# An encoder block on one core: other buffers for gates and w_out, another order for the last routed tile

## The chip, the core and the metric

The kernel runs on one core of one Trainium2 chip. The core has a matrix engine (TensorE, PE), VectorE (DVE), ScalarE (ACT), GpSimd (POOL) and SyncE (SP), which here issues most of the transfers; 16 DMA engines move data between the main memory and the on-chip memory. The metric is the time of one execution on the device in microseconds (us). Shown are the median of three runs of the kernel before and one profiled run.

## What is computed

One layer of an encoder block on 1024 rows of 1024 numbers: two attention branches, whose outputs are gated and merged, then a mixture of 32 experts.

```python
proj = rms_norm(x, norm_mix) @ w_in      # latents, q k v, two gates g_mla, g_diff
o_mla = mla_branch(...)
o_diff = diff_branch(...)                # needs exp(lq1 . lk1) - exp(lq2 . lk2)
merged = sigmoid(g_mla) * (o_mla @ w_mla_up) + sigmoid(g_diff) * (o_diff @ w_diff_up)
x = x + merged @ w_out
h2 = rms_norm(x, norm_ffn)
# router: best of 4 groups, then best 2 of the 8 experts in it, for each row
x = x + sum(combine[:, e] * ((silu(h2 @ w_gate[e]) * (h2 @ w_up[e])) @ w_down[e]) for e in range(32))
```

## The kernel before

Every product in full precision is made of three matmuls (`mm3`, L85 to L89) on operands split into a high part (ScalarE, L83) and a low remainder (VectorE, L84). A weight slab is 128 x 1024 numbers, 512 KB. Slabs are loaded by SP into raw buffers: five called `er`, which serve the whole kernel in turn, some called `ex` for expert weights (`N_MORE` of them), and pairs from a pool called `ring` whose tiles hold other things before.

The stages, with their place in the span:

- Projections, up to about 253 us. Then attention, up to 677 us. `gates()` computes the 32 blocks of gate columns as filler between the attention matmuls: each block is evicted by ScalarE into `sg` and stored to `g_d` by a DMA that ScalarE issues (L494 to L496). `sg` has one buffer. At the start of attention the products of lq and lk are formed from small tiles `lq` and `lj` (L607 to L615, loads on GpSimd); the first differential head has its values loaded from `dv_d` into er(3) and er(4) (L630, GpSimd).
- Merge, to about 770 us: 8 column blocks (L787 to L815). `uhi` and `ulo` are the split weights, `sgl` the gates loaded back from `g_d`. Four slabs of w_out are loaded and split within it (`slab`), the last four (k = 4 to 7, `woh` and `wol`) after it. The raw buffer of slab k is er(2 + k % 3) by `load_wo`, so k = 7 takes the buffer that k = 4 leaves.
- w_out, residual and router, to 895 us: eight tiles of 128 rows (L1024 to L1053) in an order written out by hand for TensorE, VectorE and ScalarE. A tile has two column halves of 24 matmuls (`out_mm`); between its own matmuls stand the transposes (`x2_turn`), router products (`logits`), counting (`count`, in `route`) and placing (`place`) of the tile before. For each tile SP stores the sum to `out` and the normed rows to `h2_d` (`h_d` in the trace). Expert slabs are loaded beside it, `load_pairs(2)` after every second tile.
- Experts, to the end. `slot_lists` writes the row numbers `ids` (VectorE, L1063). The first three gather buffers are cleared by ScalarE (L1084), since a gather leaves rows without a token as they are. Per expert: an indirect load of 112 rows of `h_d` (GpSimd, L1111, up to 12 ahead), eight transposes (`tokens`), 24 matmuls (`gate_up`), `hidden_t`, 12 matmuls (`down`), and an indirect store that adds 112 rows to `out` (L1163). Each add waits for the one before. `weights` splits six slabs per expert and then reloads the buffer it has read, or, for ring pairs, gives the pair to the gather or output buffers while more than `R_RAW` slabs are on their way (L1091 to L1107).

Within TensorE, VectorE and ScalarE's queues and within SP's and GpSimd's each instruction waits for those ahead of it.

Of the kernel before, what the change touches and what calls it, by code (L numbers as in the profile page):

```python
# [22 lines left out]
D = 1024  # L23
NT = 8
# [13 lines left out]
NYB = 3  # L38
N_MORE = 4
GB = 9  # L40
# [8 lines left out]
def kernel(ctx: ExitStack, tc: tile.TileContext, a, out):  # L49
# [45 lines left out]
    nlam = cst.tile([P, 1], F32, name="nlam")  # L95
    pos = cst.tile([P, NT, 2], F32, name="pos")
    eid = cst.tile([P, NT, 2], F32, name="eid")
    c4 = cst.tile([P, NT, 2, 4], F32R, name="c4")
    slots = cst.tile([P, P], F32, name="slots")
    nc.gpsimd.iota(slots, pattern=[[1, P]], base=0, channel_multiplier=0, allow_small_or_imprecise_dtypes=True)  # L100
    dump = cst.tile([P, 1], F32, name="dump")
    nc.gpsimd.iota(dump, pattern=[[0, 1]], base=S, channel_multiplier=1, allow_small_or_imprecise_dtypes=True)
    ndump = cst.tile([P, 1], F32, name="ndump")
    nc.vector.tensor_scalar(ndump, dump, -1.0, None, op0=ALU.mult)
    cnt = cst.tile([P, NE], F32, name="cnt")

# [367 lines left out]
    def gates():  # L474

        for b in range(2 * KD):
            raw = er(0)
            nc.sync.dma_start(raw, a["w_gate"][b].rearrange("p k n -> p (k n)"))
            w = []
            for j in range(2):  # L480
                w.append([pg.tile([P, 512], F32R, name=n_, bufs=3) for n_ in ("whi", "wlo")])
                split(*w[j], raw[:, j * 512:(j + 1) * 512])
            for half in range(2):
                ps = bank(gate_bank[0])
                if len(gate_bank) > 1:
                    gate_bank.append(gate_bank.pop(0))
                o = half * 512
                for k in range(KD):
                    wh, wl = w[k // 4]
                    c = slice(k % 4 * P, (k % 4 + 1) * P)  # L490
                    mm3(ps, wh[:, c], wl[:, c], hTh[k][:, o:o + 512], hTl[k][:, o:o + 512], k == 0, k == KD - 1)
                    if k < KD - 1:
                        yield
                sg = pg.tile([P, 512], F32, name="sg", bufs=1)  # L494
                nc.scalar.activation(sg, ps, AF.Copy)  # L495
                nc.scalar.dma_start(g_d[b, :, o:o + 512], sg)  # L496
                yield
# [109 lines left out]

    lq = p2.tile([P, 4, DHD], F32, name="lq")
    for i, n_ in enumerate(("lq1", "lk1", "lq2", "lk2")):
        nc.gpsimd.dma_start(lq[:, i, :], bcast(a[n_], DHD))  # L610
    lj = p2.tile([P, DHD], F32, name="lj")
    ls = p2.tile([P, 2], F32, name="ls")
# [166 lines left out]
    def load_wo(hi, lo):  # L779
        raw = er(2 + len(wo) % (N_RAW - 2))  # L780
        nc.sync.dma_start(raw, a["w_out"][:, len(wo), :])
# [38 lines left out]
    es_ps.close()  # L820
    es_r = ExitStack()
    psF = es_r.enter_context(tc.tile_pool(name="psF", bufs=4, space=PSUM))
    pwo = es_r.enter_context(tc.tile_pool(name="pwo", bufs=1, **left))
# [61 lines left out]
    def out_mm(t, c, k0, k1):  # L885
# [8 lines left out]
        for k in range(k0, k1):  # L894
            c_ = slice(k * P, (k + 1) * P)
            mm3(ps, mT[t // 2][0][:, t % 2, c_], mT[t // 2][1][:, t % 2, c_], wo[k][0][:, o], wo[k][1][:, o], k == 0, k == KD - 1)

    def weighted(t, c):

# [3 lines left out]
    def x2_half(t, c):  # L903
# [9 lines left out]
        weighted(t, 1)  # L913
        nc.sync.dma_start(out[t * P:(t + 1) * P, :], x2)
        r = rt("r2", [P, 1])
# [4 lines left out]
    def normed(t):  # L920

        h2 = PS2.pop(t)[2]
        nc.scalar.activation(h2, h2, AF.Copy, scale=R2[t])
        nc.sync.dma_start(h2_d[t * P:(t + 1) * P, :], h2)

# [95 lines left out]
    for i in range(N_MORE):  # L1021
        load([pex.tile([P, 1024], F32, name=f"ex{i}")])
    with tc.manual_schedule(engines={mybir.EngineType.PE, mybir.EngineType.DVE, mybir.EngineType.Activation}):
        for t in range(NT):  # L1024
            if 1 < t + 1 < NT:
                residual(t + 1)
            out_mm(t, 0, 0, 3)
            if t:
                x2_turn(t - 1, 0)
                x2_turn(t - 1, 1)  # L1030
                normed(t - 1)
            out_mm(t, 0, 3, KD)
            if t:
                logits(t - 1, 0, KD)
            x2_half(t, 0)
            out_mm(t, 1, 0, 6)
            if t:
# [5 lines left out]
            if t:  # L1043
                place(t - 1)
            x2_half(t, 1)
            if t % 2:
                load_pairs(2)
        logits(t, 0, 4)
        x2_turn(t, 1)
        logits(t, 4, KD)  # L1050
        normed(t)
        acted = route(t)
# [4 lines left out]
    def slot_lists(ps, n, nm):  # L1057


        idf = cst.tile([P, n], F32, name=f"idf{nm}")  # L1060
        nc.vector.tensor_scalar(idf, ps[:, 3 * n:4 * n], ndump, dump, op0=ALU.mult, op1=ALU.add)
        ids = cst.tile([P, n], I32, name=f"ids{nm}")
        LISTED.append(nc.vector.tensor_tensor(ids, ps[:, :n], idf, op=ALU.add))  # L1063
        w = cst.tile([P, n], F32, name=f"wsl{nm}")
        nc.vector.tensor_copy(w, ps[:, n:2 * n])
# [14 lines left out]
    pe = ctx.enter_context(tc.tile_pool(name="pe", bufs=1, **left))  # L1080
    gbuf = [pe.tile([P, D], F32, name=f"g{i}") for i in range(NGB)]
    with tc.issue_after(acted.ins):
        for g_ in gbuf:
            nc.scalar.activation(g_.rearrange("p (k n) -> p k n", n=P), slots[:, None, :].to_broadcast([P, KD, P]),  # L1084
                                 AF.Copy, scale=0.0)
    gused = {}
# [243 lines left out]
```

## Time and profile before

| | |
|---|---|
| median of 3 runs | 1274.68 us (1271.69 to 1276.09) |
| profiled run | 1274.59 us |
| its span, first to last instruction | 1272.4 us |
| mean granted TensorE clock | 0.966 |
| PE busy | 1158.7 us, 91% of the span |
| DVE busy | 946.0 us, 74% |
| ACT busy | 746.7 us, 59% |
| POOL busy | 172.8 us, 14% |
| moved by DMA | 228.62 MB, mean 180 GB/s |

Busy times are sums over the whole span; the stages have different limits. A granted clock of 1.00 is 2.4 GHz, 0.50 is 1.2 GHz. The duration of one matmul in the profile overlaps that of the next; the distance between two starts is the time that one costs. In brackets stand the idle time of the engine before the instruction and what ended it. A line marked SPq or ACTq is an instruction of that engine's queue that issues a transfer; its duration is that of the issue.

### The profile page before, as it was taken

To read this page: it belongs to the slowest core of one execution; us is meant where nothing else is said; L and a number is where in the kernel's file an instruction comes from. 1 tells how busy PE (TensorE), PEld (TensorE's weight loads), DVE (VectorE), ACT (ScalarE), POOL (GpSimd) and SP (SyncE) were. 2 spreads that over 40 slices of the span, in tenths; PEclk is the share of its full clock that TensorE was granted. 3 is DMA by queue.
4 is the path that set the end of the run, shared out by engine and by line. 5 is a ranking of instruction groups with operands and counts; after the bars stand their busy time and mean duration, and the time that the engine had idled before them with its cause. 6 is when DMAs were issued, how large, how long until landed. Compare 5 with 4: busy or idle time off the path is not lost.

```text
span 1272.4 us, 18235 instructions
## 1 busy us (share of the span) xinstructions
PE 1158.7 (91%) x6105; PEld 946.7 (74%) x6105; DVE 946.0 (74%) x2099; ACT 746.7 (59%) x1400; POOL 172.8 (14%) x147
## 2 busy tenths in 40 slices
PE   7889999989999998999999999999399998788993
PEld 6778888868888886778777877888277766566772
DVE  4776783458888788888865775565599988778992
ACT  5544562356667677776663443323488877667881
POOL 1000000010000001111100000000155233423112
PEclk9989999999999999999999998999599999899997
DMA  8753475383232233431125446544769999999983
GB/s 254 230 176 108 116 195 161 101 181 94 81 92 75 75 112 88 116 116 51 66 95 195 141 140 254 184 166 156 235 209 338 298 316 319 311 301 332 355 302 51
DMA packets 107615, 228.62 MB, mean 180 GB/s; under 512 B 13984, under 2 KB 47392, under 8 KB 107520
## 3 DMA queue, kind: packets, MB, share of 16 engines
q1 hardware_dynamic: 81664, 193.59, 46.0%
q0 software_dynamic: 21248, 25.46, 9.7%
q10 hardware_dynamic: 4608, 8.39, 1.8%
q8 instruction: 49, 0.80, 0.3%
q14 instruction: 46, 0.38, 0.1%
HBM read 187.53 MB, written 52.43 MB: 189 GB/s over the span
## 4 chain that ended last, share of the span: by engine, by line
PE 47%; DMA 27%; DVE 12%; ACT 6%; issue 5%; POOL 1%; SPq 1%; POOLq 0%; ACTq 0%; DVEq 0%
PE pG L87 5%; PE pG L88 5%; PE pG L89 5%; DMA ring<-in_w_exp 5%; DMA ex<-in_w_exp 4%; DMA er<-in_w_exp 4%; PE pB L530 3%; DMA out<-ring,ids 3%; DMA sgl<-g_d 2%; PE pF L87 2%; PE pF L88 2%; PE pF L89 2%; PE pO L89 2%; DVE nbd L518 2%; PE pO L87 2%
## 5 line engine op out<-in xcount | busy, mean ns | idle before, releaser
L521 ACT ACTIVATE pd<-pA,nbd 128x512 f32<-128x512 f32 (+7 forms) x128 | 94.5, 739 | 39.1 <-DVE nbd L518 36.2
L87 PE MATMUL pG<-ring,whi 128*128 128x512 f32 x240 | 98.9, 412 | 4.8 <-ACT sg L495 4.7
L518 DVE TENSOR_REDUCE nbd<-pA 128x1 f32<-128x128 f32 (+7 forms) x128 | 95.7, 749 | 2.5 <-PE pA L569 1.5
L89 PE MATMUL pG<-ring,wlo 128*128 128x512 f32 x240 | 96.0, 400 | 0.0
L88 PE MATMUL pG<-ring,whi 128*128 128x512 f32 x240 | 95.7, 399 | 0.0
L84 DVE TENSOR_TENSOR elo<-er,ehi 128x1024 fp32r<-128x1024 f32 x70 | 82.9, 1221 | 8.6 <-ACT ehi L83 8.5
L84 DVE TENSOR_TENSOR elo<-ring,ehi 128x1024 fp32r<-128x1024 f32 x66 | 78.2, 1221 | 5.8 <-ACT ehi L83 5.8
L83 ACT ACTIVATE ehi<-er 128x1024 fp32r<-128x1024 f32 x70 | 72.4, 1057 | 16.5 <-DMA er<-in_w_exp 8.9
L83 ACT ACTIVATE ehi<-ring 128x1024 fp32r<-128x1024 f32 x66 | 69.0, 1059 | 17.1 <-PE pO L89 5.2
L84 DVE TENSOR_TENSOR elo<-ex,ehi 128x1024 fp32r<-128x1024 f32 x56 | 66.8, 1222 | 12.6 <-ACT ehi L83 12.4
L83 ACT ACTIVATE ehi<-ex 128x1024 fp32r<-128x1024 f32 x56 | 58.3, 1058 | 21.2 <-DMA ex<-in_w_exp 9.6
L87 PE MATMUL pG<-ehi,xh 128*112 128x512 f32 x128 | 53.2, 416 | 19.1 <-ACT xh L83 19.1
L530 PE MATMUL pB<-ident,pd 128*128 128x128 f32 x432 | 66.0, 277 | 1.9 <-DVE pd L573 0.9
L530 PEld LDWEIGHTS pB<-ident,pd 128*128 128x128 f32 x432 | 48.8, 141 | 12.5 <-PE pO L597 2.5
L89 PE MATMUL pB<-ehi,ehl 128*112 128x512 f32 x128 | 54.1, 423 | 3.4 <-DVE ehl L84 3.3
L87 PEld LDWEIGHTS pG<-ring,whi 128*128 128x128 f32 x240 | 45.6, 190 | 15.0 <-ACT sg L495 8.8
L87 PE MATMUL pB<-ehi,ehh 128*112 128x512 f32 x128 | 53.7, 420 | 0.7 <-DVE ring L1162 0.7
L1163 POOL DMA_INDIRECT out<-ring,ids x20 | 34.1, 1706 | 138.8 <-ACT esg L1134 45.0
L89 PEld LDWEIGHTS pG<-ring,wlo 128*128 128x128 f32 x240 | 45.8, 191 | 9.2 <-DVE wlo L84 0.2
L88 PE MATMUL pB<-elo,ehh 128*112 128x512 f32 x128 | 52.5, 410 | 0.0
L89 PE MATMUL pG<-ehi,xl 128*112 128x512 f32 x128 | 52.2, 408 | 0.0
L87 PE MATMUL pO<-ehi,xh 128*112 128x512 f32 x128 | 51.6, 403 | 0.6 <-ACT ehi L83 0.6
(395 smaller groups left out, 3574.9 us busy)
## 6 DMA issues: line engine op xcount, KB each, us to landing
er<-in_w_exp SPq DMA_DIRECT2D x70, 512.0 KB
ring<-in_w_exp SPq DMA_DIRECT2D x66, 512.0 KB
ex<-in_w_exp SPq DMA_DIRECT2D x56, 512.0 KB
er<-in_w_gate SPq DMA_DIRECT2D x16, 512.0 KB
g_d<-sg ACTq DMA_DIRECT2D x32, 256.0 KB
sgl<-g_d SPq DMA_DIRECT2D x32, 256.0 KB
er<-in_w_dqkv SPq DMA_DIRECT2D x8, 512.0 KB
xT<-in_xT SPq DMA_DIRECT2D x16, 256.0 KB
```

Of the source, the lines that this page charges most:

```text
L83: nc.scalar.activation(hi, src, AF.Copy)
L84: return (eng or nc.vector).tensor_tensor(lo, src, hi, op=ALU.subtract)
L87: nc.tensor.matmul(ps, ah, bh, start=start, stop=False)
L88: nc.tensor.matmul(ps, ah, bl, start=False, stop=False)
L89: nc.tensor.matmul(ps, al, bh, start=False, stop=stop)
L518: nc.vector.tensor_reduce(nb, ps[:, :n], axis=AX, op=ALU.max, negate=True)
L521: nc.scalar.activation(p[:, :n], ps[:, :n], AF.Exp, bias=nb, accum_out=s)
L530: nc.tensor.transpose(pt[:, (b - b0) * P:(b - b0 + 1) * P], p[:, b * P:(b + 1) * P], ident)
L1163: nc.gpsimd.indirect_dma_start(out=out[:, :], out_offset=bass.IndirectOffsetOnAxis(ap=idx[:BT, :], axis=0), in_=y[:BT, :], in_offset=None, ...
```

## The change

- `sg` gets a second buffer.
- `lq` and `lj` are no longer tiles of their own; they use er(4) and er(3).
- The last slab of w_out (k = 7) is loaded into er(0).
- `pos`, `eid`, `cnt`, `c4`, `slots` and the lists of slots move to another pool; the iota of `slots` then runs before the w_out stage. There are three `ex` buffers instead of four.
- Tiles 0 and 1: TensorE first takes slabs k = 0 to 3 for both halves of both tiles, then the rest.
- Tile 7: the store to `h2_d` is issued first, then the store to `out` and the last two ring pairs.
- The first gather buffer is cleared by ScalarE in tile 1's turn, the other two right after the last tile's routing, ahead of the splits of expert slabs.

```diff
-N_MORE = 4
+N_MORE = 3
...
-                sg = pg.tile([P, 512], F32, name="sg", bufs=1)
+                sg = pg.tile([P, 512], F32, name="sg", bufs=2)
...
-    lq = p2.tile([P, 4, DHD], F32, name="lq")
+    lq = er(4)[:, :4 * DHD].rearrange("p (i n) -> p i n", n=DHD)
...
-    lj = p2.tile([P, DHD], F32, name="lj")
+    lj = er(3)[:, :DHD]
...
-        raw = er(2 + len(wo) % (N_RAW - 2))
+        raw = er(0 if len(wo) == KD - 1 else 2 + len(wo) % (N_RAW - 2))
...
+    def stored(t):
+        nc.sync.dma_start(out[t * P:(t + 1) * P, :], X2[t])
...
-        nc.sync.dma_start(out[t * P:(t + 1) * P, :], x2)
+        if t < NT - 1:
+            stored(t)
...
-        nc.sync.dma_start(h2_d[t * P:(t + 1) * P, :], h2)
+        return nc.sync.dma_start(h2_d[t * P:(t + 1) * P, :], h2)
...
+    def cleared(tile_):
+
+        return nc.scalar.activation(tile_.rearrange("p (k n) -> p k n", n=P), slots[:, None, :].to_broadcast([P, KD, P]),
+                                    AF.Copy, scale=0.0)
+
+    gbuf = [pex.tile([P, D], F32, name="g0")]
...
+        for t in range(2):
+            for c in range(2):
+                out_mm(t, c, 0, 4)
         for t in range(NT):
+            k0 = 4 if t < 2 else 0
...
-            out_mm(t, 0, 0, 3)
+            out_mm(t, 0, k0, max(k0, 3))
...
-            out_mm(t, 0, 3, KD)
+            out_mm(t, 0, max(k0, 3), KD)
...
-            out_mm(t, 1, 0, 6)
+            out_mm(t, 1, k0, 6)
...
+            if t == 1:
+                cleared(gbuf[0])
             x2_half(t, 1)
-            if t % 2:
+            if t % 2 and t < NT - 1:
                 load_pairs(2)
...
-        normed(t)
+        written = normed(t)
+        with tc.issue_after(written.ins):
+            stored(t)
+            load_pairs(2)
...
-    gbuf = [pe.tile([P, D], F32, name=f"g{i}") for i in range(NGB)]
+    gbuf += [pe.tile([P, D], F32, name=f"g{i}") for i in range(1, NGB)]
     with tc.issue_after(acted.ins):
-        for g_ in gbuf:
-            nc.scalar.activation(g_.rearrange("p (k n) -> p k n", n=P), slots[:, None, :].to_broadcast([P, KD, P]),
-                                 AF.Copy, scale=0.0)
+        for g_ in gbuf[1:]:
+            acted = cleared(g_)
```

SP's queue at the last tile, before. `h_9934` are the normed rows of tile 7, `out<-xr` the sum of tile 7, `ring` and `er` expert slabs:

```order
L924 DMA h_d<-h_9796 128x1024
L870 DMA ring<-in_w_exp 128x1024
L914 DMA out<-xr 128x1024
L870 DMA ring<-in_w_exp 128x1024 x3
L924 DMA h_d<-h_9934 128x1024
L870 DMA er_8991<-in_w_exp 128x1024
```

After:

```order
L928 DMA h_d<-h_9796 128x1024
L928 DMA h_d<-h_9934 128x1024
L899 DMA out<-xr 128x1024
L870 DMA ring<-in_w_exp 128x1024 x4
L870 DMA er_8991<-in_w_exp 128x1024
```

The store of the last normed rows has moved ahead of one store and four ring loads.

ScalarE's queue behind the routing of the last tile, before; `ex<-dl` is the routing's last instruction, `ehi` are expert slabs, `g` gather buffers:

```order
L976 ACTIVATE ex<-dl 128x1
L83 ACTIVATE ehi<-er_8991 128x1024
L83 ACTIVATE ehi<-er_8993 128x1024
L83 ACTIVATE ehi<-er_8995 128x1024
L83 ACTIVATE ehi<-er_8997 128x1024
L83 ACTIVATE ehi<-er_8999 128x1024
L83 ACTIVATE ehi<-ex_9001 128x1024
L83 ACTIVATE ehi<-ex_9003 128x1024
L1084 ACTIVATE g_10176<-slots 128x1024
L1084 ACTIVATE g_10177<-slots 128x1024
L1084 ACTIVATE g_10178<-slots 128x1024
```

After:

```order
L980 ACTIVATE ex<-dl 128x1
L1030 ACTIVATE g_10176<-slots 128x1024
L1030 ACTIVATE g_10177<-slots 128x1024
L83 ACTIVATE ehi<-er_8991 128x1024
L83 ACTIVATE ehi<-er_8993 128x1024
```

Two clears stand ahead of the splits, where three stood behind seven of them.

TensorE's queue at the start of tile 0, before; `slab` are the first four slabs of w_out, `woh` and `wol` the last four, the number behind `pF` tells the column half (9014 and 9042 are those of tile 0):

```order
L89 MATMUL pF_9014<-slab0_8732,ring_8144 128x512
L87 MATMUL pF_9014<-woh_8939,ring_8143 128x512
L88 MATMUL pF_9014<-wol_8940,ring_8143 128x512
L89 MATMUL pF_9014<-woh_8939,ring_8144 128x512
L87 MATMUL pF_9014<-woh_8945,ring_8143 128x512
```

After (9013 and 9026 are the halves of tile 0, 9042 and 9055 those of tile 1):

```order
L89 MATMUL pF_9013<-slab0_8726,ring_8138 128x512
L87 MATMUL pF_9026<-slab0_8429,ring_8137 128x512
...
L89 MATMUL pF_9055<-slab0_8726,ring_8138 128x512
L87 MATMUL pF_9013<-woh_8939,ring_8137 128x512
L88 MATMUL pF_9013<-wol_8940,ring_8137 128x512
```

The first matmul on `woh` stands behind 48 matmuls on the first four slabs, where it stood behind 12.

## Rows read from the trace of the kernel before

**Rows 1.** Windows: us, length, busy us per engine (instructions), TensorE clock, DMA share, GB/s.
```profile
770.60:802.40 31.80, 28.97 (x125) 22.59 (x124) 17.12 (x53) 9.32 (x17) 1.02 (x4) 0.89 0.66 254
802.40:816.50 14.10, 14.10 (x79) 11.83 (x78) 8.00 (x35) 3.67 (x9) 0.55 (x1) 1.00 0.77 261
945.00:1233.00 288.00, 263.86 (x1243) 196.29 (x1242) 252.32 (x292) 219.55 (x270) 92.50 (x47) 0.97 0.96 321
```

**Rows 2.** Timeline of ScalarE, gates to merge: start, us, line, operation, [idle before <-releaser].
```profile
678.11 0.60 ACT L495 ACTIVATE sg<-pG 128x512 f32<-128x512 f32 x1 [5.12 <-DMA g_d<-sg]
```

**Rows 3.** Timeline of TensorE in attention and at the merge's start; distance of starts is the step.
```profile
273.98 0.44 PE L567 MATMUL pA<-x,x 104*128 104x384 f32 x1 [1.81 <-ACT pd L521]
...
276.64 0.40 PE L87 MATMUL pG<-ring,whi 128*128 128x512 f32 x1
276.87 0.40 PE L88 MATMUL pG<-ring,whi 128*128 128x512 f32 x1
...
679.87 0.80 PE L87 MATMUL pG<-oth,uhi 128*128 128x512 f32 x1 [2.86 <-ACT uhi L83]
680.46 0.63 PE L88 MATMUL pG<-otl,uhi 128*128 128x512 f32 x1
680.89 0.63 PE L89 MATMUL pG<-oth,ulo 128*128 128x512 f32 x1
```

**Rows 4.** Timeline of SP, ScalarE and TensorE, the slab k = 7 of w_out.
```profile
748.83 0.33 SPq L870 DMA_DIRECT2D er<-in_w_exp  x1
...
773.41 0.33 SPq L781 DMA_DIRECT2D er<-in_w_out  x1
...
777.12 1.06 ACT L83 ACTIVATE woh<-er 128x1024 fp32r<-128x1024 f32 x1 [3.16 <-DMA er<-in_w_out]
...
779.49 0.79 PE L88 MATMUL pF<-wol,ring 128*128 128x512 f32 x1 [0.76 <-DVE wol L84]
```

**Rows 5.** Timeline of TensorE, routing of the last tile.
```profile
893.26 0.19 PE L995 MATMUL pG<-M,tri 128*128 128x32 bf16 x1 [2.81 <-DVE M L981]
...
894.78 0.91 PE L1013 MATMUL pO<-L,sl 128*128 128x128 f32 x2 [1.31 <-DVE sl L1012]
```

**Rows 6.** Timeline of all engines, last tile to first gather.
```profile
892.92 4.83 ACT L83 ACTIVATE ehi<-er 128x1024 fp32r<-128x1024 f32 x5
...
896.08 0.19 DVE L1063 TENSOR_TENSOR ids<-pO,idf 128x32 int32<-128x32 f32 x1
...
899.55 2.94 ACT L1084 ACTIVATE g<-slots 128x1024 f32<-128x1024 f32 x3
900.88 1.12 POOL L1111 DMA_INDIRECT g<-h_d,ids  x1 [11.26 <-ACT g L1084]
...
911.45 1.73 PE L1119 MATMUL pA<-ident,g 112*128 112x112 f32 x8 [15.70 <-DMA g<-h_d,ids]
```

**Rows 7.** Chain of waits in that stretch: start, us, what.
```profile
890.82 8.10 DMA h_d<-h
...
902.30 12.01 DMA g<-h_d,ids
```

**Rows 8.** Line 1111, gathers: times from issue to landing, us.
```profile
DMA to landing us min/median/max: 3.9/11.4/15.0
```

**Rows 9.** Timeline of GpSimd and TensorE, start of attention.
```profile
173.99 0.76 POOL L630 DMA_DIRECT2D er<-dv_d  x1 [2.43 <-ACT rsn L120]
...
262.01 0.50 PE L87 MATMUL pG<-ring,whi 128*128 128x512 f32 x1 [2.08 <-ACT sg L495]
```

**Rows 10.** Timeline of SP, expert loads after the preload.
```profile
937.17 5.41 SPq L870 DMA_DIRECT2D ring<-in_w_exp  x6
```

**Rows 11.** Line 1163, scatter-adds: durations in ns, first and last start, landing times.
```profile
L1163 POOL DMA_INDIRECT out<-ring,ids x20: 1462/1518/3071, 981.0 to 1260.2; - x20
L1163 POOL DMA_INDIRECT out<-y,ids x12: 1462/1542/8500, 941.7 to 1247.6; - x12
...
DMA to landing us min/median/max: 5.5/9.1/13.2
```

More of the change, by code (lines that the diff above doesn't have):

```diff
@@ L95 @@
     nlam = cst.tile([P, 1], F32, name="nlam")
[L96 to L100, printed above, removed]
     dump = cst.tile([P, 1], F32, name="dump")
@@ L104 @@
     nc.vector.tensor_scalar(ndump, dump, -1.0, None, op0=ALU.mult)
-    cnt = cst.tile([P, NE], F32, name="cnt")
     def rstd(dst, ss, width):
@@ L821 @@
     es_r = ExitStack()
+    pos = pex.tile([P, NT, 2], F32, name="pos")
+    eid = pex.tile([P, NT, 2], F32, name="eid")
+    cnt = pex.tile([P, NE], F32, name="cnt")
+    c4 = pex.tile([P, NT, 2, 4], F32R, name="c4")
+    slots = pex.tile([P, P], F32, name="slots")
+    nc.gpsimd.iota(slots, pattern=[[1, P]], base=0, channel_multiplier=0, allow_small_or_imprecise_dtypes=True)
     psF = es_r.enter_context(tc.tile_pool(name="psF", bufs=4, space=PSUM))
@@ L1057, in slot_lists @@
     def slot_lists(ps, n, nm):
-        idf = cst.tile([P, n], F32, name=f"idf{nm}")
+        idf = pex.tile([P, n], F32, name=f"idf{nm}")
         nc.vector.tensor_scalar(idf, ps[:, 3 * n:4 * n], ndump, dump, op0=ALU.mult, op1=ALU.add)
-        ids = cst.tile([P, n], I32, name=f"ids{nm}")
+        ids = pex.tile([P, n], I32, name=f"ids{nm}")
         LISTED.append(nc.vector.tensor_tensor(ids, ps[:, :n], idf, op=ALU.add))
-        w = cst.tile([P, n], F32, name=f"wsl{nm}")
+        w = pex.tile([P, n], F32, name=f"wsl{nm}")
         nc.vector.tensor_copy(w, ps[:, n:2 * n])
```

## The prediction

> **What bounds the kernel now.** I first read the windows by stage. Tile 0 and 1 of the w_out stage take 31.80 us with TensorE busy for 28.97 at a mean clock of 0.89, while a steady tile takes 14.10 us with TensorE busy throughout at 1.00. In the expert stage (945 to 1233 us) the DMA engines are busy 0.96 of the time, and VectorE 252 of 288 us [rows 1]. So the attention, merge and w_out stages go as fast as TensorE is fed, and the expert stage as fast as weights come in. Then I read the timeline at each place that the diff touches, for what arrives last there; last the landing times of the indirect transfers and the chain of scatter-adds that ends the kernel. The profiled run is 1274.59 us, its span 1272.4, and the median 1274.68: the trace stands for the median, and I count from 1274.6.
>
> **Two gate buffers.** The last eviction of gate columns on ScalarE waits 5.12 us for the store of the buffer that it is to fill [rows 2], and the splits of the first merge weights stand behind it. TensorE waits 2.86 us for these splits, until 679.87 [rows 3], so its last gate matmul ended at 679.87 - 2.86 = 677.01. With a second buffer the eviction can start there instead of at 678.11. The tail from its start to TensorE's restart is 679.87 - 678.11 = 1.76 us, so TensorE restarts at about 678.8: 1.06 us won, and 1.80 idle. Behind the old gap the clock is at its lower level (1.2 GHz): the steps from one matmul to the next are 0.43 us, against 0.23 at 2.4 GHz. A gap of 1.81 us at 273.98 is followed by steps of 0.23 [rows 3]. Eight matmuls ran slow, 8 x 0.2 = 1.6 us. Won: 1.1 if the clock falls again, 2.7 if it holds. The row nearest in length says that it holds; I take 2. For the other 30 gate blocks I cost the buffer at nothing: they are filler between attention matmuls and hide their stores.
>
> **w_out for tiles 0 and 1.** The slab k = 7 is loaded late: its issue at 773.41 waits for the buffer that slab k = 4 held, its split runs at 777.12, and TensorE idles for it, at the end for 0.76 us [rows 4], after other waits for the splits. The changed kernel puts it in er(0), which is free at 748.83 (there SP issues the first expert load into it) [rows 4]. The four woh splits still end near 777.5, since two of them and three merge splits stand in ScalarE's way, but 48 matmuls on ready slabs come first: 48 x 0.23 = 11 us from 770.6, to 781.6. So nothing waits. Two tiles' matmuls are 96 x 0.23 = 22.0 us, and the turns, logits and placing of one tile are 14.10 - 11.0 = 3.1: 25.1 without any stall, against 31.8. That is the upper bound, 6.7 us. But the matmuls pulled forward were cover for tile 0's routing. Its transposes now stand directly behind the last matmul of tile 0, so they wait for the residual add; its count stands behind 6 matmuls of a column half where there were 18, and its placing waits again. Where no matmuls cover these, for the last tile, count waits 2.81 and place 1.31 us [rows 5]. Count has 6 x 0.23 = 1.4 of cover left: 1.4 to 1.6 lost; place 1.3; the transposes between 0 and 1.3, take 0.9. Together 3.7, so the gain is 6.7 - 3.7 = 3.0. The old loss is 31.80 - 28.97 = 2.83 us of gaps and 6.7 - 2.8 = 3.9 of lower clock behind them; if one of the new gaps costs a stretch of lower clock as the gate's did (1.6 us), 1.4 is left, with two about nothing. I take 3.0, with 0 and 6.7 as bounds. The rest of the stage is TensorE work, so what is won here arrives at its end.
>
> **Last tile, clears, gathers.** Now the last h_d store is issued at 890.82 behind the out store and four ring loads, and lands 8.10 us later [rows 6, 7]. ScalarE splits seven expert slabs from 892.92 and clears the three gather buffers only from 899.55; GpSimd's first gather goes at 900.88, where the profile names the clears. The row numbers it needs are written at 896.08, which the change doesn't move [rows 6]. In the new order two clears follow routing at once (2.94 / 3 = 0.98 us each; the third is made during tile 1, where ScalarE is idle most of the time: it is busy 3.67 of the 14.10 us of a steady tile [rows 1]) and end near 893.0 + 2.1 = 895.1. The h_d store is ahead of 2.5 MB, and needs to land by 896.3: 5.5 us after its issue, against 8.10 with that load ahead of it. So the row numbers become last, at 896.3, and the first gather goes at 896.6, 4.3 us earlier. The second gather now takes 12.01 us to land beside loads [rows 7], and the 2.5 MB that were ahead of h_d are now beside them; TensorE's transposes wait for them, 15.70 us for the first until 911.45 [rows 6]. I keep that duration and take 4.0, with 0 (a gather that takes the longest landing of the trace, 15.0 [rows 8]) and 6 (one as short as 10) as bounds. The splits start 2.1 us later, at 895.1: VectorE began its part at 896.3 anyway, and the tokens arrive 11 us after that. The Trainium skill, page "DMA: Bandwidth & Descriptors", section "Issuing engines are not separate DMA queues", says that transfers of all engines interleave on the same 16 DMA engines; by it the gathers can't escape the displaced 2.5 MB whichever queue issued them, which the 12.01 us bear out.
>
> **Start of attention, a loss.** The lq rows and the scratch lj go to er(4) and er(3). The two loads of dv_d for the first head, which GpSimd issued by 173.99 into these buffers [rows 9], must now wait until the second of the products on lq is done, about 255, where VectorE comes to them. Then 1 MB moves beside the stores and loads on which the first head waits, and TensorE waits 2.08 us there already [rows 9]. On the other hand VectorE's products no longer wait for lq, whose loads now have most of the projections to arrive. Between 0 and 3 us, take 1.0.
>
> **Expert stage.** One ex buffer fewer: 24 slabs (0.52 MB each) are there when the experts begin, 25 before. A slab at 321 GB/s [rows 1] is 1.6 us. Against this the ring keeps one pair more for weights (five pairs are given to gather and output buffers, where six were), so 14 slabs circulate instead of 13. I take 0, between -2 and +3. Moved iotas and small tiles cost nothing: GpSimd idles there.
>
> **Sum:** 1274.6 - 2.0 - 3.0 - 4.0 + 1.0 + 0 = 1266.6 us.
>
> **Rivals.** (a) *The start is won and the expert stage swallows it.* SP issues loads in order, and one without a free buffer stops all behind it: after the preload it issues no ring load until 937.17, then six [rows 10]. If that stall ends no earlier than now, the stream is saturated from the same 945 us and ends where it does, 1.6 us later for the slab that is missing; some of the 8 us survives in the tail: 1271 to 1275, say 1273. For it speaks 0.96 of DMA; against it that the stalled buffers come free by splits and gathers of the first experts, which start 8 us earlier.
> (b) *Nothing stalls in tiles 0 and 1 and both clock drops go:* -2.7 - 6.7 - 4 + 1 gives 1262.
> (c) *The gathers are slowed* by the displaced 2.5 MB as far as they start earlier: the 4.0 go, 1270.6.
> (d) *Slower: the scatter-adds.* Each of the 32 waits for the one before; the first is at 941.7, the last at 1260.2 [rows 11]: 318.5 / 31 = 10.3 us a turn, of which 9.1 us (median) are landing under load. With 14 slabs circulating instead of 13 the queue ahead of each is up to 14/13 as long: 9.1 x 14/13 = 9.8, so 0.7 x 31 = 22 us at worst. Part goes into the slack of a turn; it decides from (8 + 3.8) / 31 = 0.38 us a turn upward, and at two thirds of its worst, 15, the time is 1266.6 + 15 = 1281.6. For it: the last scatter-add starts 12.2 us before the end of the span. Against: a turn of 10.3 us has 1.2 us beyond its landing, part of it waiting for the row block to add, and the landing is the same with more or fewer loads issued if the DMA engines are saturated either way. The same page of the Trainium skill, section "Queues, rings and completion order", says that each DMA engine serves its queues in turn, a packet at a time; by it the depth of the load queue would not lengthen a scatter on GpSimd's queue, and the time stays 1266.6. The landings, 5.5 to 13.2 us [rows 11], show only that load matters, not depth.
> (e) *The h_d store is not freed by the new order*, since SP or another wait holds it: this is the 0 end of the gathers' term, as (c).
>
> **How the numbers follow.** Within 0.3% is within 3.8 us, about what a measurement of this kernel can tell from no change: 1270.9 to 1278.5. Forecast, 1263 to 1270: 0.56. (a) 0.18. (b) 0.10. (c) and (e) 0.06, half of it beyond the border. (d) 0.10. Faster is 0.56 + 0.10 + 0.03 = 0.69, same 0.18 + 0.03 = 0.21, slower 0.10. The range leaves out (d) and the far end of (b): 1259 (the upper bounds of w_out and the gate, gathers at 6 and the start at 0 would give 1274.6 - 15.4 = 1259.2) to 1275 (the upper end of (a)).
>
> **What would show it.** The last gate eviction without a wait for its store and a gap under 2 us behind it with 0.23 us steps after; k = 7 issued before 755 us, tiles 0 and 1 near 28.8 us with gaps before tile 0's transposes, count and place; h_d ahead of out and gathers released by the row numbers, the first tokens turned near 903 instead of 911; the chain end 8 us earlier. Wrong if the first tokens come early and the last scatter does not: then it is (a) or (d), told apart by whether SP's loads or the scatter turns lengthened.

## The result: 8 us less, of which the terms of the forecast bring about four

The changed kernel takes 1266.67 us, the median of five runs (1263.59 to 1268.81), the kernel before 1274.68 beside it: a ratio of 0.9937, 95% interval 0.991 to 0.9963. Run again on another chip it was 0.9935 (0.991 to 0.9959). That is the forecast of 1266.6 within 0.1 us, and closer than its working deserves: one term was nearly four times its forecast, and in the two profiles of the changed kernel the four terms together come to 4.0 and 3.9 us instead of 8.0. The rest lies in stages that the forecast had put at nothing. So the nearness is luck. The profiled run of the changed kernel took 1264.64 us, 2 us under its median, its span 1262.6; I use a second profile of it (1268.21, span 1266.2) wherever one execution might mislead.

The windows answer [rows 1]; the first is tiles 0 and 1, the second a steady tile.

```profile
770.30:798.70 28.40, 26.21 (x125) 20.78 (x124) 16.85 (x53) 9.81 (x18) 1.21 (x5) 1.00 0.71 268
798.70:813.00 14.30, 14.30 (x78) 11.89 (x78) 7.81 (x35) 3.67 (x9) 0.55 (x1) 1.00 0.70 254
945.00:1233.00 288.00, 263.80 (x1241) 196.80 (x1240) 253.94 (x293) 220.57 (x270) 107.72 (x47) 0.98 0.95 320
```

Tiles 0 and 1 take 28.4 us, where they took 31.8, at a granted clock of 1.00 instead of 0.89. The DMA share of the expert stage is nearly unchanged: 0.95, where it was 0.96.

ScalarE, SP and TensorE at the two places of [rows 2], [rows 3] and [rows 4]. The first four lines are TensorE where the merge begins, the next two ScalarE's last gate eviction and SP's load of the slab k = 7, the last three the gaps in tiles 0 and 1.

```profile
679.55 0.50 PE L87 MATMUL pG<-oth,uhi 128*128 128x512 f32 x1 [1.80 <-ACT uhi L83]
679.89 0.40 PE L88 MATMUL pG<-otl,uhi 128*128 128x512 f32 x1
680.28 0.80 PE L89 MATMUL pG<-oth,ulo 128*128 128x512 f32 x1
680.87 0.63 PE L87 MATMUL pG<-oth,uhi 128*128 128x512 f32 x1
...
677.79 0.60 ACT L489 ACTIVATE sg<-pG 128x512 f32<-128x512 f32 x1 [4.84 <-PE pG L89]
...
748.55 0.33 SPq L775 DMA_DIRECT2D er<-in_w_out  x1
...
788.08 0.66 PE L935 MATMUL pB<-ident,xr 128*128 128x128 f32 x4 [0.35 <-DVE xr L911]
...
796.03 0.18 PE L999 MATMUL pG<-M,tri 128*128 128x32 bf16 x1 [1.32 <-DVE M L985]
...
798.14 0.76 PE L1017 MATMUL pO<-L,sl 128*128 128x128 f32 x2 [0.42 <-DVE sl L1016]
```

The eviction waits for TensorE alone now, and the gap is 1.80 us as forecast, but the clock fell behind it: from the third matmul to the fourth it is 680.87 - 680.28 = 0.59 us, and the following steps are 0.43. The slab is issued at 748.55. Its gaps are gone, and the three that were forecast stand in their place: transposes 0.35, count 1.32, place 0.42 us.

SP, ScalarE, VectorE, GpSimd and TensorE at the last tile, against [rows 6].

```profile
888.04 0.32 SPq L928 DMA_DIRECT2D h_d<-h  x1
888.41 0.42 SPq L899 DMA_DIRECT2D out<-xr  x1
...
890.03 0.20 ACT L980 ACTIVATE ex<-dl 128x1 f32<-128x1 f32 x1 [0.84 <-DVE dl L978]
890.14 1.99 ACT L1030 ACTIVATE g<-slots 128x1024 f32<-128x1024 f32 x2
...
893.28 0.19 DVE L1084 TENSOR_TENSOR ids<-pO,idf 128x32 int32<-128x32 f32 x1
893.76 2.16 POOL L1131 DMA_INDIRECT g<-h_d,ids  x1 [6.93 <-DMA ring<-in_w_exp]
...
902.38 1.73 PE L1139 MATMUL pA<-ident,g 112*128 112x112 f32 x8 [9.43 <-DMA g<-h_d,ids]
```

The store goes first, the clears follow the routing (890.03), and the first gather goes 3.73 us behind the routing where it went 900.88 - 892.82 = 8.06 behind it (the routing's last instruction at 892.82 stands directly ahead of the split at 892.92 in [rows 6]). It goes 0.3 us after the row numbers are written (893.28 + 0.19 = 893.47), as forecast; the line names a ring load instead, which the gather does not read.

GpSimd and TensorE at the start of attention, against [rows 9].

```profile
252.44 1.54 POOL L624 DMA_DIRECT2D er<-dv_d  x2 [88.49 <-ACT to L278]
...
262.35 0.50 POOL L539 DMA_DIRECT2D x<-in_mq  x1 [6.53 <-DMA dk_d<-to]
...
257.80 0.50 PE L87 MATMUL pG<-ring,whi 128*128 128x512 f32 x1 [0.69 <-ACT sg L489]
...
264.94 0.33 PE L563 MATMUL pA<-x,x 96*128 96x128 f32 x1 [1.23 <-DVE x L84]
...
268.78 0.79 PE L87 MATMUL pG<-ring,whi 128*128 128x512 f32 x1 [3.11 <-ACT sg L489]
269.37 0.63 PE L88 MATMUL pG<-ring,whi 128*128 128x512 f32 x1
269.80 0.63 PE L89 MATMUL pG<-ring,wlo 128*128 128x512 f32 x1
```

The two loads of dv_d go at 252.44, a load of the first heads' masks then waits 6.53 us, by the profile for the store of keys, and TensorE idles 0.69, 1.23 and 3.11 us, the last with the clock at its lower level behind it (269.37 to 269.80 is 0.43 us).

So that every run can be read in the same way, the span is cut at seven events of the timeline (us): the start of the last group of transposes of the projections on TensorE, the end of the last gate matmul, the first matmul on w_out, the router product of tile 1, the last routing instruction on ScalarE, the first matmul of expert 0, and the last scatter-add.

| profiled run | projections end at | to last gate matmul | to w_out | to tile 1's router product | steady tile | last routing to first gather | last routing to expert 0 | to last scatter-add |
|---|---|---|---|---|---|---|---|---|
| before | 254.0 | 423.0 | 93.6 | 38.25 | 14.08 | 8.06 | 22.7 | 344.7 |
| changed | 251.1 | 426.7 | 92.6 | 34.94 | 14.23 | 3.73 | 18.4 | 341.8 |
| changed, again | 251.9 | 427.0 | 92.3 | 34.93 | 14.23 | 3.73 | 18.6 | 344.6 |
| last tile undone | 252.0 | 425.8 | 93.3 | 34.94 | 14.23 | 6.78 | 20.3 | 344.7 |
| w_out undone | 251.8 | 426.9 | 92.2 | 38.19 | 14.23 | 3.73 | 17.7 | 342.1 |
| one gate buffer | 253.2 | 425.6 | 92.0 | 34.94 | 14.23 | 3.73 | 18.0 | 343.4 |
| lq in er(2) | 251.5 | 423.6 | 92.8 | 34.94 | 14.23 | 3.75 | 17.8 | 345.7 |
| 32 bytes ahead | 253.4 | 431.1 | 93.6 | 34.84 | 14.19 | 3.73 | 18.6 | 343.5 |
| gap filled | 252.0 | 428.1 | 94.7 | 34.93 | 14.23 | 3.74 | 18.9 | 344.9 |
| three halves | 254.6 | 427.0 | 93.0 | 32.47 | 14.23 | 3.74 | 18.7 | 344.5 |
| two clears late | 253.7 | 427.9 | 92.2 | 34.92 | 14.23 | 4.33 | 17.5 | 342.5 |
| lq and halves | 252.0 | 422.4 | 92.0 | 32.47 | 14.23 | 3.73 | 17.8 | 345.0 |
| h_d behind | 255.1 | 429.1 | 91.8 | 34.93 | 14.23 | 8.11 | 21.9 | 345.7 |
| clears behind | 254.9 | 426.0 | 92.5 | 34.93 | 14.23 | 5.22 | 18.9 | 342.1 |

What one column spreads over kernels that don't differ in it is the chance of one execution: the projections 251.1 to 255.1, the expert stage 341.8 to 345.7, the merge 91.8 to 93.6 (with two gate buffers, the gap not filled), from the last routing to expert 0 17.5 to 18.9 where the gather goes within 4.4 us of the routing, while the w_out columns repeat to 0.02 us. A term in the first or last column can't be told from chance by one profile; in the w_out columns 0.1 us can.

### The profile page after: what moved, and what is told of

Read it like the earlier page. It is cut to its first block, busy times and chain, and to the rows that moved or that the text cites. A ratio compares the mean times of both kernels' runs of the same rounds, so it can differ in the third digit from the quotient of the medians.

```text
span 1262.6 us, 18229 instructions
## 1 busy us (share of the span) xinstructions
PE 1156.1 (92%) x6105; PEld 944.6 (75%) x6105; DVE 945.8 (75%) x2099; ACT 746.8 (59%) x1400; POOL 188.7 (15%) x147
## 5 line engine op out<-in xcount | busy, mean ns | idle before, releaser
L84 DVE TENSOR_TENSOR elo<-ring,ehi 128x1024 fp32r<-128x1024 f32 x88 | 104.7, 1220 | 13.0 <-ACT ehi L83 12.9
L83 ACT ACTIVATE ehi<-ring 128x1024 fp32r<-128x1024 f32 x88 | 91.4, 1057 | 25.4 <-DMA ring<-in_w_exp 13.8
L84 DVE TENSOR_TENSOR elo<-er,ehi 128x1024 fp32r<-128x1024 f32 x65 | 76.9, 1220 | 11.8 <-ACT ehi L83 11.6
L83 ACT ACTIVATE ehi<-er 128x1024 fp32r<-128x1024 f32 x65 | 67.3, 1056 | 21.8 <-DMA er<-in_w_exp 12.5
L1183 POOL DMA_INDIRECT out<-ring,ids x17 | 38.0, 2238 | 116.0 <-DVE elo L84 39.6
L660 PE MATMUL pA<-x,x 128*128 128x512 f32 (+3 forms) x168 | 47.9, 370 | 5.0 <-ACT pd L515 4.8
L88 PE MATMUL pO<-elo,xh 128*112 128x512 f32 x128 | 50.4, 394 | 1.5 <-DVE elo L84 1.5
```

Of the source, the lines that this page charges most:

```text
L83: nc.scalar.activation(hi, src, AF.Copy)
L84: return (eng or nc.vector).tensor_tensor(lo, src, hi, op=ALU.subtract)
L88: nc.tensor.matmul(ps, ah, bl, start=False, stop=False)
L660: nc.tensor.matmul(ps[f][:, k], q, ks[f][j][:, k], start=j == 0, stop=j == 1)
L1183: nc.gpsimd.indirect_dma_start(out=out[:, :], out_offset=bass.IndirectOffsetOnAxis(ap=idx[:BT, :], axis=0), in_=y[:BT, :], in_offset=None, ...
```

## The experiments

Each kernel is the changed kernel with one edit, unless said otherwise. The times are medians beside runs of the kernel before on the same chip, whose own median there was 1276.5 to 1277.8 us; so ratios are compared.

### The last tile as before

```diff
-        if t < NT - 1:
-            stored(t)
+        stored(t)
...
-            if t % 2 and t < NT - 1:
+            if t % 2:
                 load_pairs(2)
...
-        written = normed(t)
-        with tc.issue_after(written.ins):
-            stored(t)
-            load_pairs(2)
+        normed(t)
...
-            if t == 1:
-                cleared(gbuf[0])
...
-        for g_ in gbuf[1:]:
-            acted = cleared(g_)
+        for g_ in gbuf:
+            cleared(g_)
```

> The changed kernel with the last tile as before: its normed rows are stored behind the out store and four ring loads, and all three gather buffers are cleared behind the splits of seven expert slabs. Theory: the last tile's part is worth what its gathers start earlier, 4.3 us, or up to 7 if their shorter landing counts too. Then the first gather is released by the clears again, about 4.3 us later than in the changed kernel as counted from the last routing (8.1 instead of 3.7 us behind the routing's last instruction on ScalarE), and the time is 1271 to 1274 us. Rival: the expert stage swallows what comes early. Then the gather is as late, but the time stays near 1267.

Ratio 0.9956 (0.9933 to 0.998), 1271.53 us: 0.2% above the changed kernel's 0.9935, inside both intervals. The gather goes 6.78 us behind the routing, and expert 0 begins 1.7 to 1.9 us later than in the two profiles of the changed kernel. The rival, that the expert stage swallows what comes early, doesn't show in its column (344.7 against 341.8 and 344.6). Not all was undone: the first buffer was still cleared ahead of the splits, as the last three runs made plain.

### w_out as before

```diff
-        raw = er(0 if len(wo) == KD - 1 else 2 + len(wo) % (N_RAW - 2))
+        raw = er(2 + len(wo) % (N_RAW - 2))
...
-        for t in range(2):
-            for c in range(2):
-                out_mm(t, c, 0, 4)
         for t in range(NT):
-            k0 = 4 if t < 2 else 0
+            k0 = 0
```

> The changed kernel with w_out as before: slab k = 7 is loaded into the buffer that slab k = 4 leaves, and tiles 0 and 1 run one after the other. Theory: tiles 0 and 1 take 31.8 us again instead of 28.4, the later tiles are as they were, and the time is 3.4 us above the changed kernel, 1270. Rival (swallowed later): tiles 0 and 1 at 31.8, the time near 1267. A further question to its trace: a steady tile takes 14.08 us in the kernel before and 14.23 in the changed one; if the order of tiles 0 and 1 makes this, it is 14.08 here.

Ratio 0.9962 (0.9939 to 0.9984), 1272.06 us. The column of tiles 0 and 1 is 38.19 us, as before (38.25); so this part is worth 3.25 us, and nothing else in it moves. The steady tile stays at 14.23: its 0.15 us don't come from the new order.

### One gate buffer

```diff
-                sg = pg.tile([P, 512], F32, name="sg", bufs=2)
+                sg = pg.tile([P, 512], F32, name="sg", bufs=1)
```

> The changed kernel with one buffer for gate columns. Theory: the second buffer is worth 1.06 us, the difference of the gaps between the last gate matmul and the first merge matmul, since the clock fell behind the shorter gap as well. So the gap is 2.86 us again (1.80 with two buffers), about eight matmuls run at steps of 0.43 us in both, and the time is 1267.7, too close to tell. Rival: the gates of the attention stage gain as well, since their evictions no longer wait for their stores; then the attention stage is longer here and the time 2 us or more above the changed kernel.

Ratio 0.9949 (0.9924 to 0.9974), 1270.71 us. The attention stage is not longer (425.6 against 426.7), so the rival falls. The gap is 2.69 us, but the clock, which had been expected to fall behind it, doesn't, and the merge is as short as nearly any. TensorE at the merge's start in this run:

```profile
681.47 0.50 PE L87 MATMUL pG<-oth,uhi 128*128 128x512 f32 x1 [2.69 <-ACT uhi L83]
...
682.53 0.39 PE L87 MATMUL pG<-oth,uhi 128*128 128x512 f32 x1
682.76 0.40 PE L88 MATMUL pG<-otl,uhi 128*128 128x512 f32 x1
```

A gap of 2.69 us leaves steps of 0.23 here; of 1.80 brings 0.43 in the changed kernel. Over all profiles, gaps of 1.8 us brought the fall in six (changed twice, last tile undone, 32 bytes, three halves, clears behind) and none in three (w_out undone, two clears late, h_d behind). The length of the gap doesn't decide alone.

### The gap filled

```diff
     for _ in gate_steps:
         pass
+    ps_ = bank()
+    for _ in range(7):
+        nc.tensor.matmul(ps_, oT[0][0][:, :P], oT[0][0][:, :512], start=True, stop=True)
     es_g.close()
```

> The changed kernel with seven matmuls more, whose result nobody reads, between the last gate matmul and the first merge matmul (7 x 0.23 = 1.6 us of the 1.80 us gap). Theory: the clock falls behind the gap in some executions (it did in the changed kernel and with the last tile undone, it didn't with w_out undone, at the same gap of 1.80), so with the gap filled it never falls here: all steps after it are 0.23, and from the last gate matmul's end to the first w_out matmul it is 92.6 - 1.6 = 91.0 us at most. Rival: the clock falls by what went before in attention; then eight steps of 0.43 can show again.

Ratio 0.994 (0.992 to 0.9961), 1271.19 us: no gain. The expectation fails: the merge takes 94.7 us from the last gate matmul, the longest of all, and not 91.0, and the fall of the clock has only moved. TensorE in this run, the first matmul of the merge's first two halves, and behind the second a window with the granted clock (0.51, ahead of the DMA figures):

```profile
681.87 0.50 PE L87 MATMUL pG<-oth,uhi 128*128 128x512 f32 x1 [0.18 <-ACT uhi L83]
...
689.42 0.50 PE L87 MATMUL pG<-oth,uhi 128*128 128x512 f32 x1 [1.76 <-DVE sgl L805]
...
690.90:694.40 3.50, 3.50 (x10) 2.71 (x9) 1.45 (x4) 1.17 (x3) 0.00 (x0) 0.51 0.48 145
```

What TensorE gains in the first half it waits for at the second: 1.76 us for VectorE's product on `sgl`, the gates loaded back, against 0.24 us in the kernel before where the first half ran slow. Behind this wait the clock falls after all, for steps of 0.43 us. Where the clock held by itself at first a wait at the same place shows too (1.18 us with w_out undone, 0.86 with two clears late), and there it held behind the wait as well. So the merge's start goes by the loads of gates, and the fall of the clock costs little there: 92.9 us is the mean of the six with it at a gap of 1.8, 92.1 of the three without, in a column that spreads by 1.8.

### lq in another buffer

```diff
-    lq = er(4)[:, :4 * DHD].rearrange("p (i n) -> p i n", n=DHD)
+    lqr = er(2)
+    lq = lqr[:, :4 * DHD].rearrange("p (i n) -> p i n", n=DHD)
...
-    lj = er(3)[:, :DHD]
+    lj = lqr[:, 4 * DHD:5 * DHD]
```

> The changed kernel with the lq rows and their scratch in er(2), which the first differential head doesn't load into, instead of er(4) and er(3). Theory: in the changed kernel the two loads of dv_d go at 252.4, and their 1 MB delays the loads of the first heads; TensorE idles 1.23 and 3.11 us there and the clock falls. With er(2) they go near 171 to 176 again, the 3.11 us gap shrinks to about 2 or less, and the time is 2 to 3 us lower, 1264. Rival: the first heads wait for loads that are late by themselves, and what the trace shows as loss is that the projections ended 2.9 us earlier by chance; then the first head starts no earlier relative to the last projection and the time stays within 1 us of 1266.7.

Ratio 0.9892 (0.9848 to 0.9935), 1264.17 us: the lowest so far. GpSimd, SP, TensorE and ScalarE in this run, then ScalarE in the kernel before:

```profile
170.52 0.77 POOL L625 DMA_DIRECT2D er<-dv_d  x1
173.38 0.77 POOL L625 DMA_DIRECT2D er<-dv_d  x1 [2.08 <-ACT rsn L114]
...
254.58 0.60 SPq L546 DMA_DIRECT2D er<-q_d  x1
...
258.98 0.33 SPq L546 DMA_DIRECT2D er<-k_d  x1
...
266.66 0.50 PE L87 MATMUL pG<-ring,whi 128*128 128x512 f32 x1 [2.01 <-ACT sg L489]
...
268.13 0.44 PE L561 MATMUL pA<-x,x 104*128 104x384 f32 x1 [0.25 <-ACT pd L515]
...
267.62 0.37 ACT L515 ACTIVATE pd<-pA,nbd 128x128 f32<-128x128 f32 x1 [1.01 <-DVE nbd L512]
...
270.93 1.06 ACT L83 ACTIVATE x<-er 96x1024 fp32r<-96x1024 f32 x1 [2.40 <-DMA er<-q_d]
...
272.52 1.06 ACT L83 ACTIVATE x<-er 96x1024 fp32r<-96x1024 f32 x1 [2.52 <-DMA er<-q_d]
...
273.49 0.35 ACT L521 ACTIVATE pd<-pA,nbd 128x128 f32<-128x128 f32 x1
```

The loads of dv_d are back at 170.52 and 173.38, and SP's first load of keys after the projections goes at 258.98 (263.17 in the changed kernel, where the projections ended 0.5 us earlier). The first scores come no earlier, 12.3 us after the end of the projections in both kernels; but to the last gate matmul it is 423.6 us, against 425.6 to 431.1 in the eleven profiles with lq in er(4). The rival, that nothing is won, falls. The stage is not shorter than in the kernel before, where it took 423.0.

The third block of the first head's scores (268.13) comes 16.6 us after the projections, against 22.8 in the changed kernel and 20.0 in the one before, but these three can't be compared as the cost of a wait: ScalarE's queue has the exponentials of the first blocks (`pd`) ahead of the split of the next q_d here, and behind it in the kernel before and in the changed one. The run changed SP's order as well: the first head's load of q_d, which also uses er(2), goes at 254.58, where the changed kernel has it at 190.50. How much of the gain is the loads of dv_d and how much these orders isn't shown apart.

### Three column halves first

```diff
-        for t in range(2):
-            for c in range(2):
-                out_mm(t, c, 0, 4)
+        for t, c in ((0, 0), (0, 1), (1, 0)):
+            out_mm(t, c, 0, 4)
         for t in range(NT):
             k0 = 4 if t < 2 else 0
+            k1 = 4 if t < 1 else 0
...
-            out_mm(t, 1, k0, 6)
+            out_mm(t, 1, k1, 6)
```

> The changed kernel with three column halves instead of four (tile 0 both, tile 1 the first) started on the first four slabs, so that tile 1's second half keeps its 24 matmuls in a row as cover for tile 0's count and placing. Theory: the gaps of 1.32 us before count and 0.42 before placing vanish (the 0.35 before the transposes stays), and 36 x 0.233 = 8.4 us still cover the last split, so tiles 0 and 1 gain 1.7 us. Rival: the last split ends only near 780, and the gap moves to the first matmul on it; then the gain is under 0.5.

Ratio 0.9934 (0.9912 to 0.9956), 1269.64 us. The column is 32.47 us, 2.46 us less than with four halves, and more than the 1.7 of the two gaps that vanish: they cost more than their idle time. The rival falls. The whole time doesn't show it, by its interval of 0.4%; in this profile the projections ended 3 us late.

### 32 bytes ahead of the slabs

```diff
     nlam = cst.tile([P, 1], F32, name="nlam")
+    pad = cst.tile([P, 8], F32, name="pad")
+    nc.vector.memset(pad, 0.0)
```

> The changed kernel with an unused tile of 32 bytes per partition ahead of all others on one side of the on-chip memory, so that the slabs of w_out (what TensorE streams) again start 32 bytes above a multiple of 64, as in the kernel before and as the ring tiles (what it holds) do in both; in the changed kernel they start at a multiple of 64. Theory: this placing makes the step of the w_out matmuls 0.228 instead of 0.233 us. Then a steady tile takes 14.08 us again (14.23 in the changed kernel and its three variants so far), 8 tiles gain 384 x 0.0055 = 2.1 us, and the time is 1264.6. Rival: something else of the change (what loads beside it, or three ex buffers) makes the step; then 14.23 stays.

Ratio 0.9962 (0.9944 to 0.9981), 1272.75 us: nothing won. The steady tile is 14.19 us: 0.04 of the 0.15 come back, so the theory falls for the most part. Attention took 431.1 us in this profile, 2 to 5.5 more than in the others with lq in er(4), and I don't know why.

### Two clears late, all clears late, the store late

The first of these three undoes the clears only, by the last two pieces of the first diff above; the second also moves the first buffer to the pool of the others, so that all three clears stand behind four splits; the third undoes the stores only, by the first three pieces.

> The changed kernel with only the clears undone: all three gather buffers are cleared behind the splits, the normed rows of the last tile are still stored first. Theory: the clears are what holds the gathers, so the first gather goes 6.8 us behind the last routing on ScalarE as with both undone, and the early store is worth nothing alone. Rival: the store held them as well; then the gather comes earlier than with both undone.

> The changed kernel with all three clears behind four splits of expert slabs, the normed rows stored first. The run with the clears undone left the first of them ahead of the splits, and its first gather went 4.3 us behind the last routing. Theory: here the first clear ends 0.1 + 4 x 0.95 + 1.04 = 4.9 us behind the routing and releases the gather, at 4.9 to 5.1, the other two follow at one us each, and TensorE's first transposes come about 1.2 us later than in the changed kernel. Rival: landing takes longer or shorter by chance than what the clears cost (8.1 to 10.6 us so far); then the first transposes don't follow the gather.

> The changed kernel with only the order of stores undone: out and four ring loads ahead of the last normed rows, the clears early. Theory: the store holds the first gather by itself, so it goes about 6.8 us behind the last routing, as with both parts undone, and not 3.7. Rival: the clears hold it (the profile of the kernel before named them); then it goes at 3.7 to 4.3.

One execution each: 1268.19, 1268.64 and 1277.63 us (the last in an execution whose stages before the last tile were late by some 5 us). With two clears late the gather goes 4.33 us behind the routing where 6.8 had been expected; the first buffer was again cleared ahead of the splits. ScalarE and GpSimd with all clears behind, then ScalarE, SP and GpSimd with the store behind, last the landing times of SP's stores to h_d in that run:

```profile
893.13 0.20 ACT L980 ACTIVATE ex<-dl 128x1 f32<-128x1 f32 x1 [0.84 <-DVE dl L978]
893.24 3.88 ACT L83 ACTIVATE ehi<-er 128x1024 fp32r<-128x1024 f32 x4
897.03 2.94 ACT L1030 ACTIVATE g<-slots 128x1024 f32<-128x1024 f32 x3
...
898.35 1.67 POOL L1128 DMA_INDIRECT g<-h_d,ids  x1 [8.42 <-DMA ring<-in_w_exp]
...
895.64 0.20 ACT L979 ACTIVATE ex<-dl 128x1 f32<-128x1 f32 x1 [0.84 <-DVE dl L977]
895.75 1.99 ACT L1029 ACTIVATE g<-slots 128x1024 f32<-128x1024 f32 x2
...
889.94 0.33 SPq L870 DMA_DIRECT2D ring<-in_w_exp  x1
890.89 0.34 SPq L899 DMA_DIRECT2D out<-xr  x1
891.28 2.26 SPq L870 DMA_DIRECT2D ring<-in_w_exp  x3
893.65 0.38 SPq L927 DMA_DIRECT2D h_d<-h  x1
...
903.75 1.18 POOL L1127 DMA_INDIRECT g<-h_d,ids  x1 [11.31 <-DMA er<-in_w_exp]
...
DMA to landing us min/median/max: 2.6/5.1/9.2
```

With the clears at 895.75 to 897.74 and the store behind out and four loads, the first gather goes at 903.75: 8.11 us behind the routing, just as in the kernel before, 6 us after the clears and 10.1 after the store's issue. This store has the longest landing of the eight, 9.2 us, so it lands near 902.9, and the gather waits for it. In the three profiles with the store first that have its landing (changed again, lq and halves, clears behind) it lands 2.6 us after its issue. Expert 0 begins 3.3 to 3.5 us later than in the changed kernel. With the store first and the clears behind four splits, the first buffer's clear ends near 898.0 and the gather goes at 898.35, 5.22 behind the routing and 1.5 later than in the changed kernel; expert 0 begins 0.3 to 0.5 us later, which is within what that column spreads. The store has most of this part, and for the clears, which the trace of before names, no worth at expert 0 is shown. In the kernel before both were late: there the store landed at 890.82 + 8.10 = 898.92, and the first clear ended at 900.5.

### Both repairs

lq in er(2), and three halves.

> The changed kernel with both repairs that the runs so far point to: lq and its scratch in er(2), and three column halves instead of four started on the first four slabs. Theory: both gains are local and add up, attention 3.4 us shorter and tiles 0 and 1 2.5 us, so it is 5 to 6 us under the changed kernel run beside it, a ratio to the kernel before of about 0.989. Rival: the expert stage swallows it, since its loads were no earlier with the three halves alone (0.9934, as the changed kernel); then it is within 2 us of the changed kernel, 0.993.

> The changed kernel itself beside the others on this chip, for a direct comparison: 0.9937 was its ratio on another chip. Theory: 0.992 to 0.996. Rival: its ratio depends on the chip as the times of the kernel before do (1274.7 on one, 1277.8 on this one), and it comes out at 0.996 or above.

Ratio 0.9882 (0.9855 to 0.9909), 1260.68 us; the changed kernel beside it 0.9935, 1267.61 us: 6.9 us less, and the intervals just don't meet. The two columns show the gains where they were made, 422.4 against 427.0 and 32.47 against 34.93, and the expert stage keeps them: 345.0 against 344.6. This is the fastest kernel here.

## Why the prediction was right, step by step

- **Bound and method:** right. What was won at any stage arrived at the end: columns of later stages don't grow when an earlier one shrinks. The expert stage took 341.8 to 345.7 us in all 14 profiles, whether expert 0 began at 901 or at 918 us.
- **Two gate buffers, 2.0 forecast:** 1.0 and 1.3 in the two profiles. The gap of 1.80 us was right to the hundredth. Wrong was the step "the row nearest in length says that it holds": the clock fell in six of nine such cases, and behind a gap of 2.69 us it didn't. Wrong as well was the price of 1.6 us: the merge waits for gates behind it, so at most 0.8 us remain. With one buffer the merge came out at 92.0 us, so the buffer's worth of about 1 us is not shown beyond the spread of that column.
- **w_out, 3.0 forecast:** 3.3 in its own column, and 3.25 by undoing it. The upper bound and the three new gaps were right in kind; they were 0.35, 1.32 and 0.42 us, 2.1 in sum instead of 3.7. But here they cost more than their idle time: the last two, 1.74 us idle, cost 2.46 by the run with three halves. And six steady tiles take 0.15 us more each, which the sum had not: 0.9 us. Until the last routing the part gave 2.5 us.
- **Last tile, 4.0 forecast:** 4.2 and 4.1 by the column to expert 0, and the first gather 4.3 us earlier, released by the row numbers, as forecast. But I had taken the clears as the holder and the store as late by less: each was late by itself, and undone alone the store costs 3.3 to 3.5 us, and the clears no more than the column's spread (0.3 to 0.5).
- **Start of attention, 1.0 lost as forecast, between 0 and 3:** 3.7 and 4.0, beyond the upper bound. The mechanism was the one named, the loads of dv_d beside those of the first heads, as far as the run with lq in er(2), which changed two orders as well, can show it; mis-sized was its term. I had set 2.08 us of idle time and the end of the wait for lq against it. That wait went down to 0.69, but nothing of this is left at the end of the stage: with lq in er(2), where neither the loads of dv_d nor the wait for lq stand in the way, it is as long as before within 0.6 us (423.6 and 422.4 against 423.0). So the buffers chosen for lq and lj cost 3 to 5 us (423.6 and 422.4 against 426.7 and 427.0), and no gain against it is shown.
- **Expert stage, 0 forecast:** -2.9 and -0.2, within its spread of 3.9. One slab fewer is not to be seen.
- **The sum:** the four terms come to 1.0 + 2.5 + 4.2 - 3.7 = 4.0 us in the first profile and 1.3 + 2.5 + 4.1 - 4.0 = 3.9 in the second, half of the 8.0 of the forecast. The expert stage adds 2.9 and 0.2, and projections that ended earlier than in the one profile of before 2.9 and 2.1. That profile's 254.0 lies inside the 251.1 to 255.1 of the others, so I take these for chance, and cannot show it, with one profile of before. The medians say 8.0, with an interval of 4.7 to 11.5. That they meet the forecast to 0.1 us is luck; where the other half comes from stays open.
- **Rivals:** (a) and (d) fell. SP's ring loads after the preload restart at 929.54 instead of 937.17 [rows 10], and the scatter-adds keep their turn: (1250.3 - 935.2) / 31 = 10.2 us, landing 9.2 us in the median of the second profile (9.1 before). (b) didn't come about: gaps and the fall of the clock both appeared. (c) fell: TensorE's first transposes come 8.6 us after the first gather (902.38 - 893.76), where it was 10.6 (911.45 - 900.88). (e) fell: the store is issued at 888.04, ahead of the others.

The lines for the last point, against [rows 8], [rows 10] and [rows 11]: SP's timeline and the scatter-adds' durations of the first profile, then the landings of scatter-adds and of gathers of the second. The first profile has the landing of only 6 of its 32 scatter-adds and 2 of its 32 gathers, the one of before of 8 each; the second has all.

```profile
929.54 8.38 SPq L870 DMA_DIRECT2D ring<-in_w_exp  x8
...
L1183 POOL DMA_INDIRECT out<-ring,ids x17: 1463/1519/6017, 969.4 to 1250.3; - x17
L1183 POOL DMA_INDIRECT out<-y,ids x15: 1463/1550/4489, 935.2 to 1243.8; - x15
...
DMA to landing us min/median/max: 5.5/9.2/13.4
...
DMA to landing us min/median/max: 4.2/10.2/14.0
```

The Trainium skill, page "DMA: Bandwidth & Descriptors", section "Queues, rings and completion order", says that each DMA engine serves its queues in turn. The scatter-adds' landing did not grow with 14 slabs in the loop, which agrees, though no run here had the number of slabs alone changed. Its section "Issuing engines are not separate DMA queues" says that transfers of all issuing engines run on the same 16 DMA engines and interleave. The start of attention agrees: with GpSimd's 1 MB beside them, SP's loads of keys went at 263.17 instead of 258.98.

## What to carry to other kernels

A buffer borrowed for a small thing must be judged by what is loaded into it next: 1 KB of lq rows a partition, in the buffers of two 0.5 MB loads, cost 3 to 5 us of attention; in the buffer beside them the stage was as long as in the kernel before. When two things hold a step, the trace names the one that comes last and hides the other; make each late by itself before giving either the credit. And when matmuls are pulled forward to cover one wait, count what they covered where they stood; taking three quarters of them forward was better than all.

## What had not been expected

- The same matmuls of w_out take 0.233 us a step in the changed kernel and 0.230 in the kernel before (means over neighbouring matmuls, interrupted steps left out), at a granted clock of 1.00 in both: 14.23 and 14.08 us a tile. Moving everything by 32 bytes gave 14.19. The order of tiles, the gate buffer and lq are excluded by the runs; what makes it stays open.
- The clock fell or held behind the same gap of 1.80 us, and held behind 2.69, in executions of nearly the same program; with that gap filled it fell behind the next one, of 1.76. What decides stays open. Whoever prices such a gap should take a chance of the fall times its cost, not one or the other.
- A median of landings can rest on very few: the first profile of the changed kernel gives 7.5 us for its gathers, from 2 of 32, where the kernel before has 11.4 from 8 [rows 8]. The second, with all 32, has 10.2, so no faster landing is shown.
